# Layer 1 of a hybrid decoder trunk: four more projections in paired form, one of them issued earlier, and another order of the output rows

## The chip, the cores and the metric

The kernel runs on one core of one Trainium2 chip. The metric is the device time of one execution in microseconds. Every run of one kernel does the same work on the same data; three runs of the kernel before gave a median of 246.49 us (246.41 to 247.32).

The names of the engines: PE is the matrix engine (PEld its weight loads, which overlap the products), DVE the vector engine, ACT the scalar engine, POOL the general-purpose engine and SP the one that issues most transfers. Each engine works through its own queue in order; an instruction that waits holds everything behind it on that engine.

## The reference

Two layers over 256 tokens of width 1024, then a final RMS norm. Each layer normalises x once, projects it through one combined matrix, runs three groups of heads and adds the projected sum back:

```python
proj = jnp.einsum('bsd,de->bse', hn, w_in)
a_q, a_k, a_v, a_g, b_x, b_g, c_q, c_k, c_v, c_g = jnp.split(proj, _in_split_points(), axis=-1)
y_a = dilated_attention(qa, ka, va)... * jax.nn.silu(a_g)      # 8 heads, 512 wide
y_b = rg_lru_branch(b_x, conv_w, ...) * jax.nn.silu(b_g)       # recurrence, 256 wide
y_c = stick_breaking_attention(qc, kc, vc)... * jax.nn.silu(c_g)   # 4 heads, 256 wide
y = jnp.concatenate([y_a, y_b, y_c], axis=-1)
return x + jnp.einsum('bse,ed->bsd', y, w_out)
```

The gate paths are a_g (512 wide, so two chunks of 256), b_g and c_g (one chunk each): the "four gate chunks" below. All of it is float32, and the result has to be close to float32, so every large product is taken in three: a high part of each operand rounded to fp32r, and the two rests.

## The kernel before

**Weights.** w_in and w_out come in chunks of 1 MB per layer, numbered by the `CH_` constants (line 44): `CH_CG` is the stick-breaking gate, `CH_BG` the recurrence's gate, `CH_AG` and `CH_AG + 1` the two dilated gate chunks, `CH_O` to `CH_O + 3` the output matrix. `load_chunk` (line 102) lets SP bring a chunk in two halves; ACT writes the high part `whi` (line 115) and DVE the rest `wlo` (line 117). `ask` keeps two chunks loaded ahead.

**A projection** (`proj_b`, line 326) multiplies a chunk of 256 columns with the 256 tokens, in two halves `b` of 128 columns. There are two forms. The plain form calls `mm3` (line 225): 24 products 256 wide per half, hi by x-hi, hi by x-lo, lo by x-hi, both halves into one PSUM bank `flat`, which the caller reads. The paired form puts x-hi and x-lo side by side, so that 8 products 512 wide (line 344) do the first two terms and 8 products 256 wide (line 341) the third; each half takes a bank of its own, ACT copies the second 256 columns to `low` (line 347) and DVE adds them to the first (line 349) into an SBUF tile. The table `PAIRED` (line 46) says which chunks take which form: none in layer 0, seven in layer 1.

**Banks.** The PSUM pool `pp` has three banks. A half in paired form holds one until DVE's add of line 349 has read it.

**The order of the work.** PE's order is that of the code (`manual_schedule` on PE alone); on the other engines the framework's scheduler sets the order. The part of layer 1 around the change runs so: the gate `CH_CG`; transposes of the first dilated probabilities; the first half of `CH_BG`; then `third` (line 661), which computes the recurrence's gates, the stick-breaking values, the first dilated values `y_c["y"]` (a `pp` bank that is held until line 677 multiplies it with its gate) and the second dilated scores; the second half of `CH_BG`; then `silu`, an ACT table load, the recurrence `lru_scan` (line 605: ACT exponentials and a logarithm, DVE products and two scans), `emit_y(rt, bg, ...)` (line 432: product with the gate, then split into `yh` and `yl`), `dil_softmax` (line 549: for each of four heads two ACT exponentials, DVE reciprocal and scaling), and the two chunks of `CH_AG`.

**The output matrix.** Each of four output tiles (two of tokens by two of columns) is summed from two halves of `y`, four row blocks of 128 each. The first half holds the recurrence's blocks in places 0 and 1 and the stick-breaking ones in places 2 and 3; the second half the dilated ones. `out_mm` (line 682) runs the three terms over the four blocks. In layer 1 the last tile's second column half is summed in a bank that held `CH_AG + 1` before and that ACT seeds with x (line 692).

Of the kernel before, what the change touches and what calls it, by code (L numbers as in the profile page):

```python
# [9 lines left out]
F32 = mybir.dt.float32  # L10
# [5 lines left out]
P = 128  # L16
S = 256
# [25 lines left out]

CH_AV, CH_CV, CH_CQ, CH_CK, CH_BX, CH_CG, CH_BG, CH_AG, CH_O = 0, 2, 3, 4, 7, 10, 11, 12, 14
CH_AQ, CH_AK = (5, 8), (6, 9)
PAIRED = ((), (CH_CQ, CH_CK, CH_AQ[0], CH_AK[0], CH_BX, CH_AQ[1], CH_AK[1]))


@with_exitstack
def trunk_kernel(ctx: ExitStack, tc: tile.TileContext, x, first_x, first, wpack, prm_d, gatew, gains, consts, rope, out):  # L50
# [6 lines left out]
    sb = ctx.enter_context(tc.tile_pool(name="sb", bufs=1))  # L57
    wk = ctx.enter_context(tc.tile_pool(name="wk", bufs=2))
    pp = ctx.enter_context(tc.tile_pool(name="pp", bufs=3, space=bass.MemoryType.PSUM))
# [3 lines left out]
    def bank(pool, tag):  # L63
        return pool.tile([P, 512], F32, name=tag, tag=tag)

    def scr(w):
        return wk.tile([P, 512], F32, name="scr", tag="scr", bufs=SCR)[:, 0:w]
# [3 lines left out]
    def dep(inst, on):  # L71
        tc.add_manual_dep(inst.ins, on.ins.name, nosync)
        return inst
# [3 lines left out]
    def table(name, behind=()):  # L77
        load = act.preload_act_table_set(name)  # L78
        for u in (*loaded["users"], *behind):
            dep(load, u)  # L80
        loaded["load"], loaded["users"] = load, []
# [6 lines left out]
    def v2(a, n=2):  # L88
        return a.rearrange("p (b t) -> p b t", b=n)
# [40 lines left out]
    def weights(l, c, ahead=AHEAD):  # L130
        ask(l, c, ahead)
        return ready.pop((l, c))
# [16 lines left out]
    for k in range(NK):  # L149
# [10 lines left out]
        w = st[:, S:1024]  # L160
# [67 lines left out]
    last = {}  # L228
# [82 lines left out]
    for l in range(L):  # L311
# [14 lines left out]
        def proj_b(c, mid=None, to=None, sc=1.0):  # L326
            pair = c in PAIRED[l]
            hi, lo = [a.rearrange("p (k c) -> p k c", c=256) for a in weights(l, c, AHEAD - 1 if mid else AHEAD)]
            if pair:
                flat = None if to is not None else scr(512)  # L330
                to = [v2(flat)[:, b, :] for b in range(2)] if to is None else to
            else:
                flat = bank(pp, "pp")
            for b in range(2):
                cs = slice(b * P, b * P + P)
                if pair:
                    ps = bank(pp, "pp")
                    seq = [(b ^ i, k) for i in range(2) for k in range(NK)]
                    for i, (is_lo, k) in enumerate(seq):
                        if is_lo:  # L340
                            pe.matmul(ps[:, 0:S], lo[:, k, cs], xh[:, k, :], start=i == 0, stop=i == len(seq) - 1,  # L341
                                      skip_group_check=True)
                        else:
                            pe.matmul(ps, hi[:, k, cs], xx[:, k].rearrange("p h t -> p (h t)"), start=i == 0,  # L344
                                      stop=i == len(seq) - 1, skip_group_check=True)
                    low = wk.tile([P, S], F32, name="low", tag="low", bufs=2)
                    act.activation(low, ps[:, S:2 * S], AF.Copy, scale=sc)  # L347
                    if sc == 1.0:
                        dve.tensor_add(to[b], ps[:, 0:S], low)
                    else:  # L350
                        dve.scalar_tensor_tensor(to[b], ps[:, 0:S], sc, low, ALU.mult, ALU.add)
                else:
                    mm3(flat[:, b * 256:(b + 1) * 256], [lambda k, a=a: a[:, k, cs] for a in (hi, lo)],
                        [lambda k, a=a: a[:, k, :] for a in (xh, xl)], range(NK), b == 0, True, True)
                if b == 0 and mid:
                    mid()
                    ask(l, c)
            return flat

        def proj_to(dst, c, mid=None, sc=1.0):  # L360
            if l > 0 and c in PAIRED[l]:
                proj_b(c, mid, [dst[:, b, :] for b in range(2)], sc)
# [40 lines left out]
        vc = sb.tile([P, NT, 256], F32, name="vc", tag="vc")  # L403
# [19 lines left out]
        def silu(dst, ps):  # L423
            sg = v2(scr(512))
            src = v2(ps)
            if l == 0:
                src = v2(scr(512))
                scaled(src, ps)
            tab(sg, src, AF.Sigmoid)
            dve.tensor_mul(dst, src, sg)  # L430

        def emit_y(src, gate, k0, n):
            dst = v2(scr(n * S), n)
            dve.tensor_mul(dst, src, gate)  # L434
            yh, yl = [v[:, k0 % 4:k0 % 4 + n, :] for v in ys[k0 // 4]]
            act.activation(yh, dst, AF.Copy)  # L436
            dve.tensor_sub(yl, dst, yh.bitcast(F32))
# [4 lines left out]
        def values(vt, wts, h0, y=None):  # L442
            y = bank(yp, "y") if y is None else y
            for p in (0, 2):
                for s0, o in ((0, 0), (1, 128)):
                    for i in (p, p + 1):
                        hr, _, hs = head(h0 + i)
                        pe.matmul(y[hr, p * 128 + o:p * 128 + 256], vt[:, s0, hs], wts[i][s0],  # L448
                                  start=s0 == 0, stop=s0 == 1)
            return v2(y)  # L450
# [122 lines left out]
        rt = sb.tile([P, 2, S], F32, name="rt", tag="rt")  # L573
        it = sb.tile([P, 2, S], F32, name="it", tag="it")
        th = sb.tile([P, 2, S], F32, name="th", tag="th")
        bg = sb.tile([P, 2, S], F32, name="bg", tag="bg")
        cg = sb.tile([P, 2, S], F32, name="cg", tag="cg")
# [61 lines left out]
        sw_t, sw_heads = turned_tile()  # L639
# [20 lines left out]

        def third():
            lru_gates()
            emit_y(values(vc, sw_heads, 0), cg, 2, 2)
            y_c["y"] = values(va, pts, 0, bank(pp, "pp"))
            y_c["s"] = dil_scores(4)

# [1 line left out]
        y_half(1)  # L668
        table(LN_EXP)
        lru_scan()  # L670
        emit_y(rt, bg, 0, 2)
        dil_softmax(y_c["s"])
        ag = sb.tile([P, 4, S], F32, name="ag", tag="ag")
        ps = proj_b(CH_AG)
        table(SIGM)
        silu(ag[:, 0:2, :], ps)
        emit_y(y_c["y"], ag[:, 0:2, :], 4, 2)
        seeded = proj_b(CH_AG + 1)
        silu(ag[:, 2:4, :], seeded)
        table(LN_EXP)  # L680

        def out_mm(ps, w, t, half, ks, first, last, c0=0, c1=512, skip=False):
            v = [a.rearrange("p (k c) -> p k c", c=512) for a in w]
            ts_ = slice(t * P, t * P + P)
            mm3(ps, [lambda k, a=a: a[:, k, ts_] for a in ys[half]],
                [lambda k, a=a: a[:, k, c0:c1] for a in v], ks, first, last, skip)

        o_ps = {}
# [4 lines left out]
        for n2 in range(2):  # L693
            w = weights(l, CH_O + n2)
            for t in range(NT):
                if l > 0 and (t, n2) == (1, 1):
                    tail = [(bank(yp, "y")[:, 0:LATE], 0, LATE), (seed, LATE, 512)]
                    for ps, c0, c1 in tail[::-1]:
                        out_mm(ps, w, t, 0, range(4), c0 == 0, False, c0, c1, c0 > 0)
                    continue  # L700
                o_ps[t, n2] = bank(at, "s") if (t, n2) == (0, 0) else bank(pp, "pp")
                out_mm(o_ps[t, n2], w, t, 0, range(4), True, False)
                if (t, n2) == (0, 0):
                    y_c["p"] = dil_transposes(4)
                if (t, n2) == (0, 1):
                    emit_y(values(va, y_c["p"], 4), ag[:, 2:4, :], 6, 2)
# [57 lines left out]
def _pack_weights(w_in, w_out):  # L764
    wp = np.empty((L, NCH, P, 2048), np.float32)
    narrow = ((CH_CV, 3072), (CH_BX, 2048), (CH_BG, 2304), (CH_AG, 1536), (CH_AG + 1, 1792), (CH_CG, 3328),
              (CH_CQ, 2560), (CH_CK, 2816), (CH_AQ[0], 0), (CH_AQ[1], 256), (CH_AK[0], 512), (CH_AK[1], 768))
    yk = (4, 5, 6, 7, 0, 1, 2, 3)
    for l in range(L):
        wi = w_in[l].reshape(NK, P, 3584)  # L770
        for h in range(2):
            wp[l, CH_AV + h] = wi[4 * h:4 * h + 4, :, 1024:1536].transpose(1, 0, 2).reshape(P, 2048)
        for c, col in narrow:
            blk = wi[:, :, col:col + 256]
            if c in CH_AQ + CH_AK:
                blk = blk.reshape(NK, P, 4, 2, 32).transpose(0, 1, 3, 2, 4).reshape(NK, P, 256)
            wp[l, c] = blk.transpose(1, 0, 2).reshape(P, 2048)
        wo = w_out[l].reshape(NK, P, D)
        for h in range(2):
            for n in range(2):  # L780
                blk = np.stack([wo[k, :, n * 512:n * 512 + 512] for k in yk[4 * h:4 * h + 4]])
                wp[l, CH_O + 2 * h + n] = blk.transpose(1, 0, 2).reshape(P, 2048)
    return wp
# [56 lines left out]
```

## Time and profile before

| What | Value |
|---|---|
| median of three runs | 246.49 us (246.41 to 247.32) |
| the profiled execution's own time | 246.08 us |
| its span, first to last instruction | 244.2 us |
| PE busy | 237.5 us (97%) |
| PEld busy | 212.1 us (87%) |
| DVE busy | 195.7 us (80%) |
| ACT busy | 171.5 us (70%) |
| mean granted PE clock | 0.994 |

The table is of one execution, the profiled one; 1.9 us of its time lie outside the span. Busy times of different engines overlap, so they don't add up to the span. A row of the timeline gives the start in us from the span's beginning, the length, the engine, the line of the kernel, the operation, the tile written and the tile read, how many instructions were merged into the row, and in brackets how long the engine had stood idle before and on whom it waited. The ends of products are modelled and reach some 0.16 us into the next one; the distance from one start to the next is the safer measure. ACT and DVE overlap neighbouring instructions a little too.

### The profile page before, as it was taken

The numbers are of one execution on the slowest core, as the hardware profiler recorded it, in microseconds if no ns is written. First come the engines' busy times: TensorE is split into PE (matmuls) and PEld (weight loads), VectorE is DVE, ScalarE is ACT, GpSimd is POOL, SyncE is SP. The second block draws the span as 40 slices with busy tenths as digits, with TensorE's granted clock in tenths as the row PEclk, the third lists the DMA queues.
The fourth block names the chain that finished last, engine by engine and source line by source line (L and its number), as shares of the span: only waits on it lengthen the run. The fifth ranks groups of instructions, "written<-read, shape, count | busy, mean of one in ns | idle before, by whom it ended". The sixth has DMA issues, their size and how long they took to land.

```text
span 244.2 us, 4755 instructions
## 1 busy us (share of the span) xinstructions
PE 237.5 (97%) x1747; PEld 212.1 (87%) x1747; DVE 195.7 (80%) x468; ACT 171.5 (70%) x372; POOL 11.3 (5%) x43
## 2 busy tenths in 40 slices
PE   8999999999999999999999999999999999999991
PEld 4788999999998899878888888888889889987881
DVE  4794789999999888986594675999999967885262
ACT  4669989628688499974663775876579749993143
POOL 0037100002000000000000000000010000000000
PEclk9999999999999999999999999999999999999997
DMA  7989989455836832277358388606470762000013
GB/s 211 395 262 386 381 274 309 167 192 182 274 120 217 300 112 77 87 217 274 113 154 262 114 268 269 212 15 191 156 215 27 238 257 86 0 3 0 0 53 121
DMA packets 14038, 43.90 MB, mean 180 GB/s; under 512 B 1728, under 2 KB 3008, under 8 KB 14016
## 3 DMA queue, kind: packets, MB, share of 16 engines
q1 hardware_dynamic: 13248, 42.43, 51.6%
q10 hardware_dynamic: 576, 0.66, 0.7%
q0 software_dynamic: 192, 0.52, 0.7%
q8 instruction: 14, 0.23, 0.4%
q14 instruction: 8, 0.07, 0.1%
HBM read 42.03 MB, written 1.05 MB: 176 GB/s over the span
## 4 chain that ended last, share of the span: by engine, by line
PE 94%; DMA 3%; ACT 1%; SPq 0%; issue 0%; DVE 0%; DVEq 0%
PE pp L225 48%; PE pp L344 10%; PE s L225 9%; PE pp L341 6%; PE s L181 4%; PE s L484 3%; DMA st<-first 3%; PE y L448 2%; PE pp L383 2%; PE s L537 2%; PE pp L181 2%; PE s L464 1%; PE y L225 1%; PE pp L448 1%; PE s L596 1%; PE s L273 1%
## 5 line engine op out<-in xcount | busy, mean ns | idle before, releaser
L117 DVE TENSOR_TENSOR wlo<-st,whi 128x512 fp32r<-128x512 f32 x128 | 81.6, 682 | 9.1 <-ACT whi L115 8.7
L115 ACT ACTIVATE whi<-st 128x512 fp32r<-128x512 f32 x130 | 72.5, 627 | 13.0 <-PE pp L225 6.8
L225 PE MATMUL pp<-xx,whi 128*128 128x256 f32 x480 | 63.6, 285 | 0.0
L225 PEld LDWEIGHTS pp<-xx,whi 128*128 128x128 f32 x480 | 59.7, 191 | 1.3 <-issue 0.3
L225 PE MATMUL pp<-xx,wlo 128*128 128x256 f32 x240 | 33.7, 283 | 0.0
L225 PEld LDWEIGHTS pp<-xx,wlo 128*128 128x128 f32 x240 | 31.0, 192 | 0.0
L344 PE MATMUL pp<-xx,whi 128*128 128x512 f32 x112 | 27.2, 392 | 0.0
L344 PEld LDWEIGHTS pp<-xx,whi 128*128 128x128 f32 x112 | 20.5, 188 | 3.9
L84 ACT ACTIVATE pr<-scr,mn 128x128 f32<-128x128 f32 (+1 forms) x32 | 14.1, 442 | 6.6 <-DVE mn L544 6.6
L78 ACT ACT_TABLE_LOAD x13 | 16.7, 1283 | 1.9 <-PEq L833 1.7
L341 PEld LDWEIGHTS pp<-xx,wlo 128*128 128x128 f32 x112 | 14.5, 191 | 1.0 <-ACT scr L84 0.3
L341 PE MATMUL pp<-xx,wlo 128*128 128x256 f32 x112 | 15.3, 285 | 0.0
L225 PE MATMUL pp<-whi,yh 128*128 128x512 f32 (+1 forms) x48 | 13.3, 382 | 0.0
L225 PE MATMUL pp<-wlo,yh 128*128 128x512 f32 (+1 forms) x48 | 12.8, 372 | 0.0
L225 PE MATMUL pp<-whi,yl 128*128 128x512 f32 (+1 forms) x48 | 12.8, 372 | 0.0
L181 PE MATMUL s<-whi,xx 128*128 128x512 f32 (+1 forms) x36 | 9.8, 392 | 0.4 <-ACT whi L167 0.4
L436 ACT ACTIVATE yh<-scr 128x512 fp32r<-128x512 f32 x8 | 5.1, 632 | 7.2 <-DVE scr L434 7.1
L225 PEld LDWEIGHTS pp<-whi,yl 128*128 128x128 f32 x48 | 8.6, 188 | 1.6
L225 PEld LDWEIGHTS pp<-wlo,yh 128*128 128x128 f32 x48 | 8.6, 188 | 1.6
L225 PEld LDWEIGHTS pp<-whi,yh 128*128 128x128 f32 x48 | 8.3, 188 | 1.6 <-issue 0.3
L544 DVE CUSTOM_DVE_ANT_0 scr<-s,con 128x128 f32<-128x128 f32 (+1 forms) x32 | 9.2, 350 | 0.0
L347 ACT ACTIVATE low<-pp 128x256 f32<-128x256 f32 x14 | 5.3, 378 | 5.5 <-PE pp L344 4.7
(188 smaller groups left out, 368.4 us busy)
## 6 DMA issues: line engine op xcount, KB each, us to landing
st<-w_pack SPq DMA_DIRECT2D x66, 512.0 KB, 5.3
st<-first SPq DMA_DIRECT2D x7, 512.0 KB, 6.3
xres<-x_in SPq DMA_DIRECT2D x4, 256.0 KB, 6.9
gw_t<-gate_w SPq DMA_DIRECT2D x2, 256.0 KB, 6.4
gn<-gains SPq DMA_DIRECT2D x2, 256.0 KB, 5.7
xs<-xc POOLq DMA_DIRECT2D x4, 128.0 KB, 4.3
gf<-gains SPq DMA_DIRECT2D x2, 256.0 KB, 6.0
out<-st ACTq DMA_DIRECT2D x2, 192.0 KB, 2.6
```

The costliest lines, as they stand in the source:

```text
L78: load = act.preload_act_table_set(name)
L84: i = dep(act.activation(*a, **k), loaded["load"])
L115: split[l, c] = act.activation(h, part, AF.Copy)
L117: dve.tensor_sub(r, part, h.bitcast(F32))
L181: pe.matmul(ps[t][:, c0:c1], a[:, k, t * P:(t + 1) * P], b, start=k == 0 and all(m[0] is not ps for m in seq[:i]), stop=k == NK - 1 and al ...
L225: pe.matmul(ps, a(k), b(k), start=first and i == 0, stop=last and i == len(seq) - 1, skip_group_check=skip)
L341: pe.matmul(ps[:, 0:S], lo[:, k, cs], xh[:, k, :], start=i == 0, stop=i == len(seq) - 1, skip_group_check=True)
L344: pe.matmul(ps, hi[:, k, cs], xx[:, k].rearrange("p h t -> p (h t)"), start=i == 0, stop=i == len(seq) - 1, skip_group_check=True)
L347: act.activation(low, ps[:, S:2 * S], AF.Copy, scale=sc)
L448: pe.matmul(y[hr, p * 128 + o:p * 128 + 256], vt[:, s0, hs], wts[i][s0], start=s0 == 0, stop=s0 == 1)
L484: pe.transpose(tp[:, i * P:(i + 1) * P], tiles[h0 + h][:, j * P:(j + 1) * P], ident)
L544: dve.tensor_tensor_reduce(xs[:, cs], sps[h][:, cs], nmask[:, cs], -0.125, 3e38, ALU.add, ALU.min, mn[:, t:t + 1])
```

## The change

All four gate chunks of layer 1 take the paired form. In layer 1 the first dilated gate chunk is issued ahead of `dil_softmax` instead of behind it (in layer 0 it stays behind). The row blocks of the first half of `y` change places: stick-breaking in 0 and 1, recurrence in 2 and 3, with the packed output matrix to match, and three of the four first-half output tiles run their three terms over blocks 0 and 1 and then over blocks 2 and 3. The bank that is seeded is now the one of the second half of `CH_AG + 1`.

```diff
-PAIRED = ((), (CH_CQ, CH_CK, CH_AQ[0], CH_AK[0], CH_BX, CH_AQ[1], CH_AK[1]))
+PAIRED = ((), (CH_CQ, CH_CK, CH_AQ[0], CH_AK[0], CH_BX, CH_AQ[1], CH_AK[1], CH_CG, CH_BG, CH_AG, CH_AG + 1))
...
-                    ps = bank(pp, "pp")
+                    ps = last["bank"] = bank(pp, "pp")
...
-            emit_y(values(vc, sw_heads, 0), cg, 2, 2)
+            emit_y(values(vc, sw_heads, 0), cg, 0, 2)
...
         lru_scan()
-        emit_y(rt, bg, 0, 2)
+        emit_y(rt, bg, 2, 2)
+        ag = sb.tile([P, 4, S], F32, name="ag", tag="ag")
+        ps = proj_b(CH_AG) if CH_AG in PAIRED[l] else None
         dil_softmax(y_c["s"])
-        ag = sb.tile([P, 4, S], F32, name="ag", tag="ag")
-        ps = proj_b(CH_AG)
+        ps = ps or proj_b(CH_AG)
         table(SIGM)
         silu(ag[:, 0:2, :], ps)
         emit_y(y_c["y"], ag[:, 0:2, :], 4, 2)
         seeded = proj_b(CH_AG + 1)
         silu(ag[:, 2:4, :], seeded)
+        if CH_AG + 1 in PAIRED[l]:
+            seeded = last["bank"]
...
-                out_mm(o_ps[t, n2], w, t, 0, range(4), True, False)
+                for ks in ((0, 1), (2, 3)):
+                    out_mm(o_ps[t, n2], w, t, 0, ks, ks[0] == 0, False)
...
-    yk = (4, 5, 6, 7, 0, 1, 2, 3)
+    yk = (6, 7, 4, 5, 0, 1, 2, 3)
```

How the instructions stand on PE in layer 1, from the second half of `CH_AG + 1` through the first output tile to the transposes of the second dilated probabilities (L484); before:

```order
L225 MATMUL pp<-xx,whi 128x256 x16
L225 MATMUL pp<-xx,wlo 128x256 x8
L225 MATMUL s<-whi,yh 128x512 x4
L225 MATMUL s<-wlo,yh 128x512 x4
L225 MATMUL s<-whi,yl 128x512 x4
L484 MATMUL s<-con,pr 128x128 x12
```

Ahead of these stand four more such pairs of rows, for the first half of `CH_AG + 1`, the two halves of `CH_AG` and the second of `CH_BG`. Now, with the tiles' numbers and the engines that a row waits for, from the second half of `CH_AG` (bank tile pp_2741) on; pp_2721 is its first half, pp_2812 and pp_2832 are the halves of `CH_AG + 1`:

```order
L341 MATMUL pp_2741<-xx_1648,wlo_2459 128x256 [waits DVE_49]
L341 MATMUL pp_2741<-xx_1648,wlo_2459 128x256 x7
L344 MATMUL pp_2741<-xx_1648,whi_2458 128x512 x8
L344 MATMUL pp_2812<-xx_1648,whi_2649 128x512 [waits DVE_49,Activation_49]
L344 MATMUL pp_2812<-xx_1648,whi_2649 128x512 x7
L341 MATMUL pp_2812<-xx_1648,wlo_2650 128x256 x8
L341 MATMUL pp_2832<-xx_1648,wlo_2650 128x256 [waits DVE_49,Activation_49]
```

Each half is now 8 rows 512 wide and 8 rows 256 wide, in a bank of its own, and the first row of each half waits until the bank is free.

DVE at the same place, in the recurrence (L616 and L618 are in `lru_scan`, L434 and L437 in `emit_y`, L555 and L557 in `dil_softmax`, L430 in `silu`); before:

```order
L616 TENSOR_TENSOR it<-it,th 128x512
L555 RECIPROCAL den<-den 128x2
L618 SCALAR_TENSOR_TENSOR rt<-av,it 128x256 x2
L557 TENSOR_SCALAR pr<-pr,den 128x128
L434 TENSOR_TENSOR scr<-rt,bg 128x512
L557 TENSOR_SCALAR pr<-pr,den 128x256
L555 RECIPROCAL den<-den 128x2
```

and now:

```order
L616 TENSOR_TENSOR it<-it,th 128x512
L555 RECIPROCAL den<-den 128x2
L618 SCALAR_TENSOR_TENSOR rt<-av,it 128x256 x2
L557 TENSOR_SCALAR pr<-pr,den 128x128
L434 TENSOR_TENSOR scr<-rt,bg 128x512
L349 TENSOR_TENSOR scr<-pp,low 128x256 x2
L557 TENSOR_SCALAR pr<-pr,den 128x256
```

The two adds that empty the banks of `CH_AG` stand directly behind the recurrence's product with its gate.

ACT, from the gate's sigmoid to the second exponential of the recurrence; before:

```order
L115 ACTIVATE whi<-st 128x512 x2
L84 ACTIVATE scr<-pp 128x512
L78 ACT_TABLE_LOAD
L84 ACTIVATE av<-rt,c_285 128x256 x2
L84 ACTIVATE pr,den<-scr,mn 128x128
L84 ACTIVATE pr,den<-scr,mn 128x256
L84 ACTIVATE pr,den<-scr,mn 128x128
L84 ACTIVATE pr,den<-scr,mn 128x256
L84 ACTIVATE th<-scr,tiny 128x512
L84 ACTIVATE pr,den<-scr,mn 128x128
L84 ACTIVATE th<-th 128x512
```

and now:

```order
L347 ACTIVATE low<-pp 128x256
L115 ACTIVATE whi<-st 128x512 x2
L84 ACTIVATE scr<-scr 128x512
L78 ACT_TABLE_LOAD
L84 ACTIVATE av<-rt,c_285 128x256 x2
L347 ACTIVATE low<-pp 128x256
L84 ACTIVATE pr,den<-scr,mn 128x128
L84 ACTIVATE pr,den<-scr,mn 128x256
L84 ACTIVATE pr,den<-scr,mn 128x128
L84 ACTIVATE th<-scr,tiny 128x512
L347 ACTIVATE low<-pp 128x256
L84 ACTIVATE th<-th 128x512
```

The copies of the second half of `CH_BG` and of both halves of `CH_AG` have been placed in the recurrence's chain; the last of them stands ahead of its second exponential (`th<-th`).

## The prediction

> **What bounds the kernel now.** I read the list of PE's waits first, then PE's timeline in layer 1. PE waited on other engines for two things in the whole span, both in the first ten microseconds:
>
> ```profile
> PE y L147 <- DVE cold L135: 1.2, 1, 1.2
> PE s L181 <- ACT whi L167: 0.4, 1, 0.4
> ```
>
> So PE bounds everything behind that, and two questions decide: how much PE work goes, and whether PE has to wait anywhere new. Around the change its timeline has no gap:
>
> ```profile
> 202.31 2.08 PE L225 MATMUL pp<-xx,whi 128*128 128x256 f32 x16
> 204.23 1.12 PE L225 MATMUL pp<-xx,wlo 128*128 128x256 f32 x8
> 205.19 2.08 PE L225 MATMUL pp<-xx,whi 128*128 128x256 f32 x16
> ...
> 208.07 2.08 PE L225 MATMUL pp<-xx,whi 128*128 128x256 f32 x16
> ...
> 213.83 0.86 PE L225 MATMUL s<-whi,yh 128*128 128x512 f32 x3
> ```
>
> The chain of work that ended last has the same stretch, from CH_BG's second half on, as one piece (start, us, what):
>
> ```profile
> 199.41 14.58 PE pp L225 x120
> ```
>
> CH_AG's halves start at 202.31 and 205.19, CH_AG+1 at 208.07, the first output tile at 213.83: a half takes 2.88 us, or 14.58 / 5 = 2.92 where CH_BG's, which follows other work, is counted in.
>
> **The paired form: what it saves.** Layer 1 has halves in this form already:
>
> ```profile
> 157.06 3.82 PE L344 MATMUL pp<-xx,whi 128*128 128x512 f32 x16
> 160.72 2.08 PE L341 MATMUL pp<-xx,wlo 128*128 128x256 f32 x16
> 162.63 1.55 PE L344 MATMUL pp<-xx,whi 128*128 128x512 f32 x6
> ```
>
> Start to start, 16 wide products take 3.66 us (0.229 each) and 16 narrow ones 1.91 (0.119). A half costs 8 x 0.229 + 8 x 0.119 = 2.78 us against 2.88: 0.10 saved, 0.8 us over eight halves. Bounds: 0 (as many columns pass in both forms) and 1.1 (against 2.92, so 0.14 a half). I take 0.8, since most halves follow each other.
> [...]
>
> Added beside PE are eight copies on ACT and eight adds on DVE:
>
> ```profile
> L347 ACT ACTIVATE low<-pp x14: 360/384/387, 144.3 to 186.5; 128x256 f32<-128x256 f32 x14
> L349 DVE TENSOR_TENSOR scr<-pp,low x4: 414/418/420, 155.2 to 185.1; 128x256 f32<-128x256 f32 x4
> ```
>
> 3.1 us on ACT and 3.3 on DVE. Those of CH_CG and CH_BG's first half cost nothing: their banks are wanted again a PE half or more later, and the work behind them is splitting of weights that are used much later. The others stand in the recurrence's chain, which nobody on PE needed before 213.83. No transfer is added or moved past another on any queue.
>
> **The new wait.** pp has three banks. From third on, y_c["y"] holds one until it meets its gate; CH_AG's halves hold the other two until DVE's add (L349). So CH_AG+1 cannot start before the add of CH_AG's first half, and that add stands on DVE behind L434, the recurrence's product with its gate. Before, CH_AG+1 took the bank that CH_BG's sigmoid and product had left long before. I follow the chain through ACT:
>
> ```profile
> 201.55 1.16 ACT L115 ACTIVATE whi<-st 128x512 fp32r<-128x512 f32 x2 [2.66 <-PE pp L225]
> 202.61 0.58 ACT L84 ACTIVATE scr<-pp 128x512 f32<-128x512 f32 x1
> 203.21 1.28 ACT L78 ACT_TABLE_LOAD   x1
> 204.50 0.91 ACT L84 ACTIVATE av<-rt,c 128x256 f32<-128x256 f32 x2
> 205.32 0.39 ACT L84 ACTIVATE pr<-scr,mn 128x128 f32<-128x128 f32 x1
> ...
> 206.58 0.49 ACT L84 ACTIVATE pr<-scr,mn 128x256 f32<-128x256 f32 x1
> ...
> 207.07 0.71 ACT L84 ACTIVATE th<-scr,tiny 128x512 f32<-128x512 f32 x1
> 207.69 0.39 ACT L84 ACTIVATE pr<-scr,mn 128x128 f32<-128x128 f32 x1
> ...
> 208.07 0.62 ACT L84 ACTIVATE th<-th 128x512 f32<-128x512 f32 x1
> ```
>
> and on through DVE:
>
> ```profile
> 206.17 0.69 DVE L613 SCALAR_TENSOR_TENSOR scr<-scr,th 128x512 f32<-128x512 f32 x1
> ...
> 208.72 0.69 DVE L616 TENSOR_TENSOR it<-it,th 128x512 f32<-128x512 f32 x1 [0.54 <-ACT th L84]
> ...
> 209.45 1.27 DVE L618 TENSOR_TENSOR_SCAN rt<-av,it 128x256 f32<-128x256 f32 x2
> ...
> 210.82 0.68 DVE L434 TENSOR_TENSOR scr<-rt,bg 128x512 f32<-128x512 f32 x1
> 211.42 0.34 DVE L557 TENSOR_SCALAR pr<-pr,den 128x256 f32<-128x256 f32 x1
> ...
> 212.33 0.68 DVE L437 TENSOR_TENSOR yl<-scr,yh 128x512 fp32r<-128x512 f32 x1
> ```
>
> In the changed kernel, by these distances from start to start: the four halves ahead save 0.4, so CH_AG runs on PE from 201.91 to 207.47. CH_BG's last product ends at 202.07. ACT then does its copy (to 202.44), two weight parts (1.06, to 203.50), the sigmoid (0.60, to 204.10), the table load (1.29, to 205.39), av (0.82, to 206.21), the copy of CH_AG's first half (0.37, to 206.58), three exponentials (1.26, to 207.84), the logarithm (0.62, to 208.46; its input, L613, comes 0.90 later than it did, at 207.76, in time), the copy of CH_AG's second half (0.37, to 208.83) and the second exponential (0.62, to 209.45). DVE starts L616 at 209.49 and, as before, L434 2.10 later, at 211.59; the add follows 0.60 later, at 212.19, and ends 0.42 later, at 212.61. PE goes on at about 212.65: it has stood for **5.2 us** since 207.47.
>
> Bounds. Were ACT ready the moment CH_AG's second half is done (207.63), copy, exponential, L616 to L434, L434 to the add, and the add would still take 0.37 + 0.62 + 2.10 + 0.60 + 0.42, with about 0.1 between engines: 211.84, a wait of 4.4. Above, I allow 0.4 more for ACT: 5.6. Behind the waiting product on PE stand both halves of CH_AG+1, the output matrix and the end of the kernel; ACT and DVE wait for CH_AG+1's copies in turn.
>
> CH_AG+1 starts 4.58 later than before (212.65 against 208.07) and saves 0.2 itself: the output matrix starts **4.4 us late**. What is late next? Nothing more that I find: the recurrence's blocks are wanted near 219.6, and yl, whose chain runs 0.8 late and which has two more softmax exponentials on ACT ahead of its split, ends near 214.4 instead of 213.01.
>
> **The order of the output rows** moves the need for the recurrence's blocks back by six products of 0.229, 1.4 us. No product waited there before, so it gains nothing in either layer; after the wait above there are some 5 us of slack anyway. It costs nothing either: the products are the same in number and shape.
>
> **The clock.** A PE that stands for 5 us is new here. The one place where it stands now is the end:
>
> ```profile
> 239.00:240.00 1.00, 0.12 (x2) 0.00 (x0) 0.36 (x1) 0.78 (x4) 0.00 (x0) 1.00 0.37 137
> 240.00:241.00 1.00, 0.00 (x0) 0.00 (x0) 0.75 (x3) 0.75 (x2) 0.00 (x0) 1.00 0.00 0
> 241.00:242.00 1.00, 0.00 (x0) 0.00 (x0) 0.00 (x0) 0.00 (x0) 0.00 (x0) 0.58 0.63 226
> ```
>
> The third number from the right is the granted clock: PE ends at 239.12, and from about 241.16 it is 0.5 (0.16 of that slice at full speed gives 0.58). So 2.0 us of standing were enough, and I expect half speed when PE goes on. What that costs, the beginning shows:
>
> ```profile
> 1.19 3.17 PE L147 MATMUL y<-cold 128*128 128x512 bf16 x7 [1.19 <-DVE cold L135]
> 4.13 1.19 PE L181 MATMUL s<-whi,xx 128*128 128x256 f32 x4
> 5.13 0.63 PE L181 MATMUL pp<-whi,xx 128*128 128x256 f32 x2
> 5.55 0.69 PE L181 MATMUL s<-whi,xx 128*128 128x256 f32 x4
> ```
>
> Seven products 512 wide took 0.42 each, and four 256 wide 0.25 each (4.13 to 5.13), twice the 0.119 above; from about 5.5 on they run at full speed. That is some 4.3 us of work at half speed, of which half is lost: **2.1 us**. Bounds: 0, if the clock holds, and 3.2, if the half speed lasts longer by the 2.0 us of delay seen at the end.
> [...]
>
> **The sum**, on the profiled execution's 246.08 us (span 244.2): +4.4 for the wait less all savings, +2.1 for the clock, 252.6 us. The median of runs, 246.49, lies 0.4 above that execution; I put the time between, at **252.8 us**.
>
> **The rivals.**
> 1. The wait comes, and the clock holds. For it: one tail is thin evidence, and the clock's delay may depend on where the idle time falls. Against: the wait is over twice the delay seen. 246.08 + 4.4 = 250.5, or 250.9 by the median (249.7 to 251.3). [...]
> 2. No wait, so not slower: the bank of CH_AG's first half is empty by 207.47, because the wait that PE names is met by an earlier add, or the add runs ahead of the chain. It decides if the add ends 5.1 us earlier than I have it. What is left is the saving: 246.49 - 0.8 = 245.7, inside what can't be told from no change (0.5%, 1.2 us). Against it: the count of banks, and DVE's queue, which has the add behind L434.
> 3. A second wait behind the first. ACT is the busiest engine beside PE there, 18.2 us of 20:
>
> ```profile
> 200.00:220.00 20.00, 20.00 (x151) 19.06 (x150) 16.72 (x46) 18.20 (x41) 0.00 (x0) 1.00 0.08 28
> ```
>
> The copies of CH_AG+1, the last sigmoid, the table load, the seed and the copies of the transposes now come after 218; were values (needed about 228) held up by 2, or the clock to drop twice, it is 255 or more. Against: by the same distances those copies are done near 224.
>
> **How the numbers follow.** The forecast 0.70, its own range 251.2 to 254.5 (wait 4.4 to 5.6, clock 0.9 to 3.2); rival 1 0.16; rival 2 0.06; rival 3 0.05; 0.03 for a shorter wait than the bound allows, 247 to 249.7. The range 249.7 to 254.6 takes in the forecast and rival 1 and leaves out the rest. Even 1.1 us saved with no wait stays under 0.5%, so of rival 2's 0.06 same has 0.05 and faster 0.01; slower has 0.94.
>
> **What would show it.** PE idle some 5 us ahead of the first L344 of CH_AG+1, released by DVE L349, and DVE's L349 right behind L434; halves of 2.78 us; a granted clock of 0.5 for some 4 us from there; nothing idle on PE behind it. I am wrong if PE runs through that place, if the wait is under 4 us, or if PE waits elsewhere for longer.

## The result and the profile after

The changed kernel takes 253.41 us (median of six runs, 253.01 to 256.41) against 246.5 for the kernel before (six runs, 246.21 to 247.32): 1.0292 times as long, 95% interval 1.0243 to 1.0342. The profiled execution took 253.01 us with a span of 250.7; 1.88 us lay outside the span before, 2.31 do now.

PE's list of waits in the changed kernel is the shortest reading of it (us in total, times, longest):

```profile
PE pp L344 <- DVE scr L349: 5.0, 1, 5.0
PE y L147 <- DVE cold L135: 1.2, 1, 1.2
```

One new wait, on one instruction, released by DVE's add of line 349. PE's timeline has it between the first and the second dilated gate chunk:

```profile
203.56 2.08 PE L341 MATMUL pp<-xx,wlo 128*128 128x256 f32 x16
205.48 2.00 PE L344 MATMUL pp<-xx,whi 128*128 128x512 f32 x8
212.46 3.75 PE L344 MATMUL pp<-xx,whi 128*128 128x512 f32 x8 [4.98 <-DVE scr L349]
216.01 2.69 PE L341 MATMUL pp<-xx,wlo 128*128 128x256 f32 x16
218.54 2.00 PE L344 MATMUL pp<-xx,whi 128*128 128x512 f32 x8
220.38 0.62 PE L225 MATMUL s<-whi,yh 128*128 128x512 f32 x2
```

Eight wide products take 1.84 us start to start where nothing disturbs them (218.54 to 220.38), so PE would have gone on at 205.48 + 1.84 = 207.32; it went on at 212.46, 5.14 later. The first eight wide products behind the wait then take 3.55 us instead of 1.84. The chain of work that ended last, which was PE alone in this stretch before, now leaves PE for ten microseconds (start, us, what):

```profile
201.95 0.39 ACT low L347
202.34 1.04 ACT whi L115 x2
203.38 0.52 ACT scr L84
...
203.91 1.28 ACT L78
...
205.21 0.91 ACT av L84 x2
206.12 0.27 ACT low L347
206.38 1.27 ACT pr L84 x6
...
208.29 0.36 ACT low L347
208.65 0.53 ACT th L84
...
209.20 0.69 DVE it L616
...
209.97 1.23 DVE rt L618 x2
...
211.38 0.60 DVE scr L434
211.98 0.35 DVE scr L349
...
212.46 3.75 PE pp L344 x8
```

And the granted clock of PE, third number from the right (1.00 is full speed), in slices of a microsecond:

```profile
209.00:210.00 1.00, 0.00 (x0) 0.00 (x0) 0.80 (x3) 1.00 (x6) 0.00 (x0) 1.00 0.00 0
210.00:211.00 1.00, 0.00 (x0) 0.00 (x0) 1.00 (x2) 1.00 (x6) 0.00 (x0) 0.80 0.00 0
...
216.00:217.00 1.00, 1.00 (x6) 0.99 (x5) 1.00 (x3) 1.00 (x2) 0.00 (x0) 0.50 0.00 0
217.00:218.00 1.00, 1.00 (x9) 1.00 (x8) 1.00 (x3) 0.29 (x2) 0.00 (x0) 0.79 0.00 0
```

It falls at about 210.6 (0.80 is 0.6 of the slice at full and 0.4 at half speed) and is back at about 217.4.

To compare kernels I use one stretch that the first stage, which waits for transfers (ACT's L161 stood 3.2 us for them in the trace of the kernel before) and moves by over a microsecond between executions (one version's two traces have the row named next at 174.37 and 175.76), does not touch: from the first row of L537 in layer 1 (the scores of the first four heads; the expectations below call it the second scores, layer 0 having had the first) to the first product of the output matrix, and from there to the last product's end. Each is the distance of two rows of one trace. The stretch begins at this row in the kernel before, and its first output product is at 213.83:

```profile
174.22 0.73 PE L537 MATMUL s<-k,q 32*128 32x128 f32 x16
```

and at this one in the changed kernel, whose first output product is at 220.38:

```profile
173.95 0.73 PE L537 MATMUL s<-k,q 32*128 32x128 f32 x16
```


| Kernel | to the first output product, us | from there to the last | ratio of times, interval |
|---|---|---|---|
| before | 39.61 | 25.29 | |
| before, run again | 39.62 | 25.30 | 0.999 (0.9964 to 1.0016) |
| the change | 46.43 | 25.27 | 1.0292 (1.0243 to 1.0342) |
| second chunk in other banks | 38.93 | 27.22 | 1.0085 (1.0067 to 1.0104) |
| handed over ahead of the recurrence | 38.94 | 25.41 | 1.0036 (1.0013 to 1.006) |
| the same again | 38.93 | 25.40 | 1.0005 (0.9981 to 1.0029) |
| handed over behind the softmax | 46.93 | 25.27 | 1.0301 (1.0249 to 1.0353) |
| wait filled, 20 products | 44.19 | 25.27 | 1.0211 (1.0163 to 1.0259) |
| wait filled, 14 products | 44.21 | 25.26 | 1.0222 (1.0178 to 1.0265) |
| wait filled, 8 products | 45.49 | 25.27 | 1.0280 (1.0222 to 1.0338) |
| two gate chunks only | 39.33 | 25.30 | 0.999 (0.9967 to 1.0013) |
| order of rows only | 39.62 | 25.29 | 0.9994 (0.9966 to 1.0023) |

All of the change's 6.82 us lie in the first stretch. One execution of the version handed over ahead of the recurrence took 475.04 us, nearly all of it inside the span; it is left out of that version's ratio, and no trace of it was kept.

### The profile page after: what moved, and what is told of

Its sections match the earlier page's. It is cut to its first block, busy times and chain, and to the rows that moved or that the text cites. A ratio compares the mean times of both kernels' runs of the same rounds, so it can differ in the third digit from the quotient of the medians.

```text
span 250.7 us, 4644 instructions
## 1 busy us (share of the span) xinstructions
PE 239.3 (95%) x1683; PEld 210.4 (84%) x1683; DVE 198.7 (79%) x476; ACT 174.2 (70%) x380; POOL 11.3 (5%) x43
## 4 chain that ended last, share of the span: by engine, by line
PE 92%; ACT 3%; DVE 2%; DMA 1%; issue 1%; SPq 0%; DVEq 0%
PE pp L225 38%; PE pp L344 15%; PE s L225 9%; PE pp L341 8%; PE s L181 5%; PE s L484 3%; PE y L448 2%; PE pp L181 2%; PE pp L383 2%; PE s L537 2%; DMA st<-first 1%; PE s L464 1%; PE y L225 1%; PE pp L448 1%; PE s L596 1%; PE s L273 1%
## 5 line engine op out<-in xcount | busy, mean ns | idle before, releaser
L344 PE MATMUL pp<-xx,whi 128*128 128x512 f32 x176 | 44.8, 404 | 5.0 <-DVE scr L349 5.0
L225 PE MATMUL pp<-xx,whi 128*128 128x256 f32 x352 | 46.6, 285 | 0.0
L225 PEld LDWEIGHTS pp<-xx,whi 128*128 128x128 f32 x352 | 43.7, 191 | 0.8 <-issue 0.3
L344 PEld LDWEIGHTS pp<-xx,whi 128*128 128x128 f32 x176 | 33.0, 195 | 12.0 <-issue 5.4
L341 PEld LDWEIGHTS pp<-xx,wlo 128*128 128x128 f32 x176 | 23.5, 196 | 1.6 <-ACT scr L84 0.3
L225 PEld LDWEIGHTS pp<-xx,wlo 128*128 128x128 f32 x176 | 22.7, 192 | 0.0
L347 ACT ACTIVATE low<-pp 128x256 f32<-128x256 f32 x22 | 8.2, 377 | 11.4 <-PE pp L344 9.9
L225 PE MATMUL pp<-whi,yh 128*128 128x512 f32 (+1 forms) x48 | 14.1, 382 | 0.0
L225 PE MATMUL pp<-wlo,yh 128*128 128x512 f32 (+1 forms) x48 | 13.6, 372 | 0.0
L225 PE MATMUL pp<-whi,yl 128*128 128x512 f32 (+1 forms) x48 | 13.6, 371 | 0.0
```

The lines of the kernel that those rows point to most:

```text
L225: pe.matmul(ps, a(k), b(k), start=first and i == 0, stop=last and i == len(seq) - 1, skip_group_check=skip)
```

## The experiments

**Is it the bank?** The two halves of CH_AG+1 take banks from the scores' pool; everything ahead of them stays, DVE's late add too.

```diff
-                    ps = last["bank"] = bank(pp, "pp")
+                    ps = last["bank"] = bank(at, "s") if c == CH_AG + 1 else bank(pp, "pp")
...
-            seeded = last["bank"]
+            seeded = bank(pp, "pp")
```

> The changed kernel, but the two halves of CH_AG+1 take banks of the scores' pool, two of which are free then, and the seeded bank is a new one of pp. ACT's and DVE's order in the recurrence stays as in the changed kernel, so the add is as late as there. Theory (it is the bank): no wait ahead of CH_AG+1 though the add still ends near 212.3; a small wait of up to 1 us may come at the transposes behind the first output tile, which want the same pool's banks: 245.7 to 247. Rival (PE waits for something that the recurrence delays, weights or gates, not for the bank): the wait of 5 us stays, 253.

PE's timeline of this kernel, from the second half of the first chunk on:

```profile
206.66 2.00 PE L344 MATMUL pp<-xx,whi 128*128 128x512 f32 x8
208.50 1.98 PE L344 MATMUL s<-xx,whi 128*128 128x512 f32 x8
...
218.61 0.66 PE L484 MATMUL s<-con,pr 128*128 128x128 f32 x4 [1.21 <-DVE scr L349]
```

and DVE's, with the recurrence's product and the two adds of the first chunk:

```profile
212.49 0.68 DVE L434 TENSOR_TENSOR scr<-rt,bg 128x512 f32<-128x512 f32 x1
213.09 0.75 DVE L349 TENSOR_TENSOR scr<-pp,low 128x256 f32<-128x256 f32 x2
```

The second chunk starts at 208.50, directly behind the first (206.66 + 1.84), some 5 us before the adds of the first chunk, for the first of which the changed kernel waited, have ended (213.84 for both). So neither its weights nor anything else of the recurrence held it: it was the bank. The wait moved: the transposes behind the first output tile want the same pool's banks, and wait for the second chunk's own adds, 1.6 us in two pieces; the expectation had allowed 1. The median was 248.32 us, 1.0085, above the 247 that the expectation allowed. The trace accounts for 1.25 of these 2 us (1.93 more behind the first output product, 0.68 less ahead of it); the rest is not explained.

**Is it the place of the add?** The first dilated chunk is handed over ahead of the recurrence; PE's order does not change by it.

```diff
+        ag = sb.tile([P, 4, S], F32, name="ag", tag="ag")
+        ps = proj_b(CH_AG) if CH_AG in PAIRED[l] else None
         lru_scan()
         emit_y(rt, bg, 2, 2)
-        ag = sb.tile([P, 4, S], F32, name="ag", tag="ag")
-        ps = proj_b(CH_AG) if CH_AG in PAIRED[l] else None
         dil_softmax(y_c["s"])
```

> The changed kernel, but in layer 1 the first dilated gate chunk is handed over ahead of the recurrence instead of behind it; on DVE the add that empties its first half's bank now stands ahead of the recurrence's products, that of its second half ahead of L616. PE's order is the same. Theory (the bank is late only because its add stands behind the recurrence): the first half's add ends near 206.5, before PE wants the bank at 207.4, and the second's near 208.9, before 210.1; PE does not wait, the clock stays at 1.0, and what is left is the saving of the paired form: 245.4 to 246.1 us, 0.8 below the kernel before. Rival (the extra copies and adds of the paired form overload ACT and DVE in this stretch wherever they stand): PE still waits 2 us or more there, 249 or more.

DVE's timeline of this version has the adds of the first chunk's two halves here (the wait in brackets is DVE's own):

```profile
207.44 0.42 DVE L349 TENSOR_TENSOR scr<-pp,low 128x256 f32<-128x256 f32 x1 [0.84 <-ACT low L347]
210.31 0.40 DVE L349 TENSOR_TENSOR scr<-pp,low 128x256 f32<-128x256 f32 x1
```

and PE's timeline, from the narrow products of both halves of CH_AG on, reads:

```profile
205.38 2.08 PE L341 MATMUL pp<-xx,wlo 128*128 128x256 f32 x16
207.29 3.82 PE L344 MATMUL pp<-xx,whi 128*128 128x512 f32 x16
210.95 2.08 PE L341 MATMUL pp<-xx,wlo 128*128 128x256 f32 x16
212.86 2.00 PE L344 MATMUL pp<-xx,whi 128*128 128x512 f32 x8
```

The two adds now end at 207.86 and 210.71, and PE, which wants the first bank at 207.29 + 1.83 = 209.12, runs through: sixteen wide products in a row, eight of them of the second chunk. The same copies and adds are in this kernel, so their number is not what makes the wait; their place is. The stretch is 38.94 us, 0.67 below the kernel before. The time was not: 246.87 us, 1.0036, above the 245.4 to 246.1 that were expected.

So it was run once more:

> The version with the first dilated gate chunk handed over ahead of the recurrence, once more, since its first time (1.0036 of the kernel before) stood above what its trace gives (0.68 us less from the scores to the first output tile). Theory (time outside the span is about 0.4 us longer than before and eats the saving, and the rest was chance in the first stage): a ratio of 0.998 to 1.002. Rival (something that the one trace does not show costs it a microsecond): 1.0025 to 1.006 again.

246.4 us against 246.44, a ratio of 1.0005 (0.9981 to 1.0029), and the stretch 38.93. The saving is in both traces, and not in the time. From the first output product on PE takes 0.1 us longer (25.4 against 25.29), which leaves less than 0.6. The time outside the span is 2.3 to 2.6 us in every execution of this version, against 1.87 to 1.96 in every one of the kernel before run again. In the second run that half microsecond takes back what the spans gain (median 244.05 against 244.5 for the kernel before beside it). In the first run the spans themselves were longer (244.5 against 244.2), so there something else inside the span cost time too; in its one trace layer 1's first scores began late, at 175.76 against 174.37 in the second run's. What the program does outside the span the profile does not show, and both stay open.

**Is it the handing over between recurrence and softmax?** The first dilated chunk is handed over behind the softmax, as before the change.

```diff
-        ps = proj_b(CH_AG) if CH_AG in PAIRED[l] else None
+        ps = None
         dil_softmax(y_c["s"])
```

> The changed kernel, but the first dilated gate chunk is handed over behind the softmax, as before the change; the paired form and the order of rows stay. On DVE the add of its first half stands two instructions behind L434, on ACT both copies behind the last exponential. Theory: the copies no longer delay the recurrence (0.6 us earlier), but the add stands later behind it: the bank is free near 212.5 to 213, the wait is 5 to 5.7 us, 253 to 254.2, so handing over between recurrence and softmax buys next to nothing. Rival (the copies inside the recurrence's chain are what makes the wait): clearly below 252.

PE's timeline of this kernel:

```profile
206.46 2.00 PE L344 MATMUL pp<-xx,whi 128*128 128x512 f32 x8
213.89 3.78 PE L344 MATMUL pp<-xx,whi 128*128 128x512 f32 x8 [5.43 <-DVE scr L349]
```

and DVE's:

```profile
212.50 0.68 DVE L434 TENSOR_TENSOR scr<-rt,bg 128x512 f32<-128x512 f32 x1
213.44 0.40 DVE L349 TENSOR_TENSOR scr<-pp,low 128x256 f32<-128x256 f32 x1
```

The wait is 0.45 us longer than in the changed kernel (5.43 against 4.98); the median, 254.16 us, can't be told from the changed kernel's. The place that the change chose is hardly better than the old one, since in both the add stands behind L434.

**What does the clock cost?** Extra products of known data into a spare bank fill the wait; they change no result.

```diff
         ps = proj_b(CH_AG) if CH_AG in PAIRED[l] else None
+        if l > 0:
+            fill = bank(at, "s")
+            for i in range(20):
+                pe.matmul(fill, ones, xx[:, i % NK].rearrange("p h t -> p (h t)"), start=True, stop=True)
```

> The changed kernel with 20 extra products 512 wide of known data into a spare bank, between the first dilated gate chunk and the second: 20 x 0.229 = 4.6 us of PE work inside a wait of 5.1. They change no result and leave nothing out. Theory (half a clock after the wait costs 2.3 us): the granted clock stays 1.0 and the second chunk takes 5.6 us instead of 7.9: 250.7 to 251.5. Rival (the wait alone costs all of it, and the lower clock in the record costs nothing): 253 to 253.6, no change.

PE's timeline, with the extra products (their line in this kernel is 677):

```profile
207.99 4.75 PE L677 MATMUL s<-xx,ones 128*128 128x512 f32 x20
213.14 2.08 PE L344 MATMUL pp<-xx,whi 128*128 128x512 f32 x8 [0.40 <-DVE scr L349]
...
218.81 0.39 PE L225 MATMUL s<-whi,yh 128*128 128x512 f32 x1
```

PE goes on as late as before, but the second chunk takes 5.67 us (213.14 to 218.81) instead of the changed kernel's 7.92 (212.46 to 220.38). The stretch falls by 2.24 us and the ratio from 1.0292 to 1.0211, 2.0 us of 246.5 (the intervals of the two ratios overlap a little; the trace is the firmer evidence). The median, 251.57 us, is just above the 251.5 that were expected at most. The clock behind the wait, third from the right again:

```profile
213.00:219.00 6.00, 5.86 (x33) 5.21 (x34) 6.00 (x16) 5.69 (x11) 0.00 (x0) 1.00 0.00 0
```

So the extra work makes the kernel faster by keeping the clock up.

Then with fewer products, so that PE stands for some of the time. With 8:

> The changed kernel with 8 instead of 20 of the extra products in the wait: 8 x 0.229 = 1.8 us filled, so PE stands for about 3.3 us. Theory (2 to 2.5 us of standing are enough for the clock to fall, as at the end of the span): it still falls in most executions, the second chunk takes 7 to 8 us, about 253. [...]

PE's timeline with 8 of them:

```profile
207.46 2.00 PE L677 MATMUL s<-xx,ones 128*128 128x512 f32 x8
212.61 3.38 PE L344 MATMUL pp<-xx,whi 128*128 128x512 f32 x8 [3.15 <-DVE scr L349]
```

and the slices of a microsecond, with the clock third from the right:

```profile
211.00:212.00 1.00, 0.00 (x0) 0.00 (x0) 1.00 (x3) 0.98 (x4) 0.00 (x0) 0.99 0.00 0
212.00:213.00 1.00, 0.39 (x1) 0.42 (x2) 1.00 (x5) 0.99 (x2) 0.00 (x0) 0.50 0.00 0
...
215.00:216.00 1.00, 1.00 (x6) 0.81 (x5) 1.00 (x3) 0.07 (x1) 0.00 (x0) 0.80 0.00 0
```

and with 14 (its windows are, in the clock's record below, pieces of 3.413 us, which lie differently in each execution):

> The same with 14 extra products: 3.2 us filled, PE stands for about 1.9 us. Theory: just under the 2.0 to 2.5 us after which the clock fell at the end of the span, so the clock holds and the second chunk takes 5.6 us, about 251; if windows run freely, single executions may still show half the clock. Rival (any wait of this size costs the clock): 252.5 or more.

PE's row behind the wait with 14 products:

```profile
212.99 2.09 PE L344 MATMUL pp<-xx,whi 128*128 128x512 f32 x8 [1.77 <-DVE scr L349]
```

and the clock there:

```profile
211.00:212.00 1.00, 0.21 (x1) 0.00 (x0) 1.00 (x4) 0.98 (x6) 0.00 (x0) 1.00 0.00 0
212.00:213.00 1.00, 0.01 (x1) 0.04 (x1) 1.00 (x3) 1.00 (x1) 0.00 (x0) 1.00 0.00 0
213.00:214.00 1.00, 1.00 (x5) 0.82 (x5) 1.00 (x6) 0.99 (x3) 0.00 (x0) 1.00 0.00 0
```

With 8, PE stands for 3.15 us and the clock falls at about 212.0, 2.5 us after the last product's end (209.46); it is back at 215.4, the second chunk takes 6.96 us, just under the expected 7, and the median is 252.62 us. With 14 PE stands for 1.77 us, the clock stays at 1.0, the second chunk takes 5.68, and the median is 251.76. The half speed lasts 3.4 us with 8 and twice that, 6.8, in the changed kernel.

The clock's own record in the traces, of which the slices are means, says more. In the changed kernel it has full speed from 5.79 to 210.59 us, half to 217.42, full to 248.14 and half from there; in the kernel before, full from 5.65 to 241.17 and half from there. The lengths between, 204.80, 6.83, 30.72 and 235.52 us, are 60, 2, 9 and 69 times 3.413, and the half speed with 8 products is, by the slices, once that. So the changes of one of these executions lie on a grid of 3.413 us, and the grid lies differently in each: counted back from the changes, its first point is 2.38 us into the changed kernel's span, 2.23 into that of the kernel before and about 0.4 into the one with 8 products. In the one piece of the grid just ahead of a fall PE had worked for 0.3 us in the changed kernel's wait and 0.9 at its end, 0.9 with 8 products, not at all in the wait of the version handed over behind the softmax (where the clock fell at 212.05, 3.6 us after the last product) and 1.4 at the end of the kernel before. With 14 products the piece around the wait, 210.14 to 213.55 by the fall at that span's end (247.68), had 1.6 us of work, and the clock stayed. So in these traces it is not the length of the standing alone that decides but where it falls, as the first rival supposed: at the ends of the spans the clock fell between 2.0 us (kernel before) and 4.7 us (8 products) after the last product.

**Do the other parts cost or save anything?** First the kernel before against itself:

> The kernel before itself, unchanged, run as if it were a change, to see what the comparison makes of two equal programs and how far the stretches of its trace move between executions. Expected: a ratio of 1.000 within 0.003; from the second scores of layer 1 (first L537 row) to the first output tile 39.6 us as in the first trace, within 0.1; the time to the end of the first stage, which waits for transfers, may move by 1 us.

0.999 (0.9964 to 1.0016), 246.2 us, and 39.62 us in the stretch: the stretch repeats to 0.01 us, and the ratio misses 1 by 0.1%. Then only CH_CG and CH_BG in paired form:

```diff
-... CH_AQ[1], CH_AK[1], CH_CG, CH_BG, CH_AG, CH_AG + 1))
+... CH_AQ[1], CH_AK[1], CH_CG, CH_BG))
```

> Only the stick-breaking gate and the recurrence's gate in paired form in layer 1, and the new order of rows; both dilated gate chunks plain and in their old place. Theory (the saving is 0.10 us a half wherever PE does not wait): no wait, 39.2 to 39.3 us from the second scores of layer 1 to the first output tile against 39.6 before, a time of 0.3 to 0.4 below the kernel before, which cannot be told from no change. Rival (the paired form's copies delay the recurrence and with it something on PE): a new wait on PE, over 39.6.

No wait, and 39.33 us in the stretch, 0.28 less than before; the time, 246.52 us, is the same. And only the order of the rows, with PAIRED as it was:

> Only the new order of the output rows and the products of the first half in two groups; no gate chunk is paired. Theory (no product waited for the recurrence's blocks before): 39.6 us from the second scores of layer 1 to the first output tile and 25.3 from there to the last product, as before; no change in time. Rival (the order costs PE something by itself, or saves a wait that the trace does not show): a change of over 0.2 us in one of the two.

39.62 and 25.29 us, a ratio of 0.9994: it does nothing by itself.

No version ran clearly faster than the kernel before. The best stretch, 38.93 us, is that of the version that hands over ahead of the recurrence (and of the one with other banks, which waits later), and its 0.7 us do not reach the time.

## Why the prediction was right

The forecast, 252.8 us, is 0.6 below the measured 253.41, within its range. By its terms:

- **The new wait** is the one named, with the releaser named: 5.14 us start to start, 5.2 forecast. The chain ran as worked out to within 0.3 us at each step: the copy of CH_BG's second half at 201.95 (forecast 202.07), the logarithm's place free at 207.66 (207.84), L616 at 209.20 (209.49), L434 at 211.29 by its row of DVE's timeline (211.59), PE at 212.46 (212.65). The profiled execution as a whole was 0.27 us ahead when layer 1's first scores began (173.95 against 174.22); reckoned from there each step is within 0.15 us of the forecast. The banks settled by the first experiment and the add's place by the second were argued in the prediction; both are shown now.
- **The clock** fell, as the chance of 0.70 had it. The cost was mis-sized by a little: 7.92 - 5.57 = 2.35 us in this execution (5.57 is what the second chunk took in other banks, 208.50 to 214.07), against 2.1: PE worked at half speed for 4.96 us (212.46 to 217.42) where the prediction took 4.3 from the start of the kernel. (The slices of that start show 1.00 only because the clock's record has its first entry at 5.65 us.) With half speed of 3.4 us instead of 6.8 it is less: 45.49 - 44.21 = 1.3 us between 8 and 14 products. The 2.35 is of one trace. The mean granted clock was 0.98 to 0.983 in three of the changed kernel's six executions, the profiled one among them, and 0.993 in the other three, whose half speed must have been shorter in all; yet their spans, 250.9 to 251.1 us, are no shorter than the 250.7, 250.8 and 253.9 of the first three. So what the clock costs in the median is not shown; all eight spans with 20 or 14 products are shorter than all six, 249.0 to 250.0.
- **The saving of the paired form** is 0.67 to 0.68 us for eight halves, against 0.8, and 0.28 for four.
- These three make up the stretch: 5.14 + 2.35 - 0.68 = 6.81, and 46.43 - 39.61 = 6.82. The forecast for it was 4.4 + 2.1 = 6.5: the saving was taken 0.1 too large and the clock 0.25 too small.
- **The order of the rows** and the copies beside PE cost and save nothing, as costed.
- **What was not in the sum** is the time outside the span, 0.43 us longer in the profiled execution: 6.5 us of span became 6.9 of time. With it the sum of 252.6 would have been 253.0, the time of the profiled execution. That this comes out to the tenth is luck: the stretch was 0.3 longer than forecast, and this execution happened to be 0.27 ahead when it began.
- **The lower end of the forecast's own range**, 251.2, does not follow from the prediction's bounds: a wait of 4.4 less the savings is 3.6, and with 0.9 for the clock, which is worked out nowhere and which no run shows (the traces have 2.35 and, with 8 products, 1.3), that gives 250.6 to 251.0. The result is far from it, so nothing hung on it.
- **Rival 1** (the clock holds) would have meant about 250.9; the filled wait, where the clock does hold, took 251.57, of which some 0.4 are the longer time outside the span in three of its four executions. **Rival 2** needed an empty bank by 207.5; the version handed over ahead of the recurrence is that case, and came out as no change, as that rival said, though the time outside the span had a part in that beside the saving's size. **Rival 3**, a second wait, did not come: from the first output product on nothing differs (25.27 against 25.29 us).

## What to carry to other kernels

A form that reads a PSUM bank out by a copy and an add trades one long hold of a bank by its consumer for holds that end wherever the scheduler puts the add: before taking it, count the banks that are held at that place and look in the draining engine's queue for what stands ahead of the add. Here a gain of 0.7 us on the bounding engine cost a wait of 5 us because the add stood behind a chain that nobody else was in a hurry for; moving the hand-over by a few lines took the wait away, though the kernel was then no faster than before the change. And price a new wait on PE with the slow restart behind it, in these traces about four tenths as much again (2.35 on 5.14, 1.3 on 3.15); a wait of 1.77 us had none.

## What was not expected of the hardware

Twenty useless products made the kernel some 2 us faster, because PE had come back from its wait at half speed. The clock fell after 2.0 us of standing at the end of the span before, 2.5 in one filled wait and 3.1 in the changed kernel, held for 4.7 at another span's end, and held through a wait of 1.77; behind the waits it stayed at half speed for 3.4 us or twice that. Its changes lie whole multiples of 3.413 us apart in the traces of both kernels, and the length of the standing alone did not tell whether it fell.

The time outside the span is 1.9 to 2.0 us in all executions of the version with two paired gates and of the kernel before run again, and in 61 of the 69 of the kernel before that were timed beside the experiments (2.1 to 2.6 in the other 8); it is 2.3 to 2.6 in all of the changed kernel. The versions with other banks, with the wait filled and with the hand-over behind the softmax show both, execution by execution. It does not go with the wait, since the version without the wait has the long one. Nothing in the profile says what it is.
